# Issue order of the value products and state products in the mLSTM heads of an encoder layer

## The chip, the core and the metric

The kernel runs on one core of a Trainium2 chip. TensorE (PE) does matrix products out of SBUF into PSUM, VectorE (DVE) and ScalarE (ACT) do elementwise work, GpSimd (POOL) does masks and powers, and SyncE (SP) issues the transfers from HBM. The metric is the time of one execution on the device in microseconds.

## The reference

One encoder layer on 512 tokens of width 1024: a gated feed-forward block, a mixer, a second feed-forward block, each between RMS norms. Half of the mixer is a short convolution; the other half is four mLSTM heads, run forward and backward, in chunks of 128 tokens (q and k of width 64, v of width 128). Cut to what matters here, for one head and one direction:

```python
D = jnp.where(causal, b[..., :, None] - b[..., None, :] + li[..., None, :], NEG_INF)
...
P = jnp.exp(D - m_t[..., None]) * jnp.einsum('bhctk,bhcsk->bhcts', q, k)
inter = jnp.exp(m_inter - m_t)
numer = inter[..., None] * jnp.einsum('bhctk,bhckv->bhctv', q, C_prev) \
    + jnp.einsum('bhcts,bhcsv->bhctv', P, v)
denom = inter * jnp.einsum('bhctk,bhck->bhct', q, n_prev) + jnp.sum(P, axis=-1)
h = numer / jnp.maximum(jnp.abs(denom), jnp.exp(-m_t))[..., None]
```

For each chunk the numerator is a sum of two products: scores `P` (128x128) with values, and queries (128x64) with the state `C_prev` that the chunks before it left. The first chunk of a direction has no state. The denominator rides along as a 129th column: `v` has a column of ones, and the state its `n`.

## The kernel before, in words

Products whose operands are weights are split into a high and a low part and run in a rounded float32 type (`float32r`); the products inside the heads are plain float32, and each of them stands in the trace as two weight loads and two matmuls, so that 32 products of a line give 64 records.

The kernel is one straight program under a scheduler that keeps each engine's instructions close to the order in which they are written; which instruction waits for which follows from the tiles that they share. PSUM is a pool of eight tiles (`ps`), each one bank of 128 x 512 float32.

The mixer runs, after its projections, in this order: `head_a(0)`, `states()`, two convolution pieces, and then for each head `h` of four: `head_a(h + 1)`, `head_b(h)`, `head_c(h - 1)`, two convolution pieces. After the last of them comes the output projection (L907), then the second feed-forward block.

- `head_a(h)`: four products of keys with queries (L801, 64 rows of the PE array deep) into one PSUM tile; two products that spread gate values over rows (L806); DVE and ACT make `E`, the weighted scores of both directions (L808, L812, L814, L818).
- `states()`: the chunk states `Cs`, from weighted keys and values (L784), once for all heads.
- `head_b(h)`: for each direction `d`, into two PSUM tiles `po_` of two chunks each: the product of `E` with values (L832, 128 rows deep) for each of the four chunks, and for three of them the product of weighted queries with the state (L834, 64 rows deep: rows 0 to 63 for even heads, 64 to 127 for odd ones), accumulated onto it. DVE then forms the denominators (L841 to L844), divides (L846, L852), ACT sums squares (L857), and the head is normalized (L859).
- `head_c(h)`: four transposes (L865), the output gate (L867) and a split into high and low part.
- a convolution piece `conv(n)`: 24 products of 128 x 128 with 512 columns (L338) with a pair of weight tiles, which ACT (L220, "cast") and DVE (L221) split out of a tile `raw` that a transfer filled. The last three of the eight pieces of `w_mix_out` are loaded at L891 and split into tiles `big`.

The lines that the change touches, in short: the loop over the four chunks `c` issued for each chunk

```python
nc.tensor.matmul(o, E[...], vv[:, c, h, :], start=True, stop=i < 0)
if i >= 0:
    nc.tensor.matmul(o, qt_pair[pr][...], Cs[es, 2 * d + pr, i, :], start=False, stop=True)
```

Of the kernel before, what the change touches and what calls it, by code (L numbers as in the profile page):

```python
# [16 lines left out]
P = 128  # L17
D = 1024
S = 512
NT = S // P  # L20
# [16 lines left out]
def encoder_kernel(ctx: ExitStack, tc: tile.TileContext, a: dict, out: bass.AP):  # L37
    nc = tc.nc
# [14 lines left out]
    def nm(s):  # L53
        uid[0] += 1
        return f"{s}_{uid[0]}"
# [4 lines left out]
    def ps():  # L60
        return psum.tile([P, 512], F32, tag="ps", name=nm("ps"))

    def t2(dt=F32):
        return t2p.tile([P, 512], dt, tag="t2", name=nm("t2"))
# [4 lines left out]
    def sm(shape, dt=F32, tag="sm"):  # L69
        return small.tile(shape, dt, tag=tag, name=nm(tag))  # L70
# [4 lines left out]
    def blk(i, n=P):  # L75
        return slice(i * n, (i + 1) * n)

    def ch(v):
        return v.rearrange("p (c t) -> p c t", t=P)
# [143 lines left out]
    def rstd(parts, n, mul, tag="rs"):  # L223
        w = parts[0].shape[1]
        acc = None
        for p_ in parts:
            t = sm([P, 4], tag=tag)
            if acc is None:
                nc.vector.tensor_scalar(out=t[:, 0:w], in0=p_, scalar1=mul / n, scalar2=mul * EPS, op0=ALU.mult, op1=ALU.add)
            else:  # L230
                nc.vector.scalar_tensor_tensor(out=t[:, 0:w], in0=p_, scalar=mul / n, in1=acc, op0=ALU.mult, op1=ALU.add)  # L231
            acc = t[:, 0:w]
        r = sm([P, 4], tag=tag)
        nc.gpsimd.tensor_tensor(out=r[:, 0:w], in0=acc, in1=nhalf[:, 0:w], op=ALU.pow)  # L234
        return r[:, 0:w]
# [335 lines left out]
    vv = vaug.rearrange("p c (h e) -> p c h e", e=DV + 1)  # L571
# [138 lines left out]
    for c in range(NT):  # L710
# [3 lines left out]
        start=True, stop=True,  # L714
# [3 lines left out]
    Cs = Cf[:, 0:12 * 129].rearrange("p (q i e) -> p q i e", q=4, i=3)  # L718
# [24 lines left out]
    qt_pair = {}  # L743
# [77 lines left out]
    def head_b(h):  # L821
        pr, e = h // 2, h % 2
        es = slice(e * DK, (e + 1) * DK)
        E = hs[h]
        hsum = t2()
        for d in range(2):
            row = 32 * d + h
            po_ = [ps(), ps()]
            for c in range(NT):
                i = c - 1 if d == 0 else 2 - c  # L830
                o = po_[c // 2][:, (c % 2) * 256:(c % 2) * 256 + 129]
                nc.tensor.matmul(o, E[:, d * 512 + c * P:d * 512 + (c + 1) * P], vv[:, c, h, :], start=True, stop=i < 0)  # L832
                if i >= 0:
                    nc.tensor.matmul(  # L834
                        o, qt_pair[pr][es, d * 512 + c * P:d * 512 + (c + 1) * P], Cs[es, 2 * d + pr, i, :],
                        start=False, stop=True,
                    )
            for g in range(2):
                pov = po_[g].rearrange("p (c e) -> p c e", e=256)
                den = sm([P, 2], tag="den")  # L840
                nc.vector.scalar_tensor_tensor(  # L841
                    out=den, in0=pov[:, :, DV], scalar=-1.0, in1=nat1[:, 2 * g:2 * g + 2, 64 + row], op0=ALU.mult, op1=ALU.max)
                nc.vector.tensor_tensor(out=den, in0=pov[:, :, DV], in1=den, op=ALU.max)
                nc.vector.reciprocal(out=den, in_=den)  # L844
                if d == 0:
                    nc.vector.tensor_tensor(  # L846
                        out=ch(hsum[:, blk(g, 256)]), in0=pov[:, :, 0:DV], in1=den.broadcast_to([P, 2, DV]), op=ALU.mult,
                    )
                else:
                    for c in range(2):  # L850
                        hc = hsum[:, blk(2 * g + c)]
                        nc.vector.scalar_tensor_tensor(  # L852
                            out=hc, in0=pov[:, c, 0:DV], scalar=den[:, c:c + 1], in1=hc, op0=ALU.mult, op1=ALU.add,
                        )
        ssq = sm([P, 4], tag="ssq")
        for c in range(NT):
            nc.scalar.activation(junk[:, 0:P], hsum[:, blk(c)], AF.Square, accum_out=ssq[:, c:c + 1])  # L857
        r = rstd([ssq], DV, 1.0, tag="den4")
        nc.vector.tensor_tensor(out=ch(hsum), in0=ch(hsum), in1=r.broadcast_to([P, NT, DV]), op=ALU.mult)  # L859
        hs[h] = hsum  # L860
# [13 lines left out]
    for h in range(NH):  # L874
        if h + 1 < NH:
            head_a(h + 1)
        head_b(h)
        if h:
            head_c(h - 1)
        conv(2 * h + 3)  # L880
        conv(2 * h + 4)
# [17 lines left out]
    for tb in range(NT):  # L899
        acc = [ps(), ps()]  # L900
        for half in range(2):
            for n, k in enumerate(MIXK):
# [3 lines left out]
                for yi, wi in ((0, 0), (0, 1), (1, 0)):  # L906
                    nc.tensor.matmul(  # L907
                        acc[half], yy[yi][:, k % 4, blk(tb)], wmo[k][wi][:, blk(half, 512)],
                        start=(n == 0 and yi == 0 and wi == 0), stop=(n == 7 and yi == 1),
# [40 lines left out]
```

## Time and profile before

| | |
|---|---|
| median of 3 timed runs | 939.66 us (939.37 to 940.58) |
| profiled execution, its own time | 939.74 us |
| span of its instructions in the trace | 938.0 us |
| TensorE busy | 926.2 us of the span, 99% |
| VectorE, ScalarE, GpSimd busy | 633.5, 417.5, 39.2 us |
| granted TensorE clock, mean | 0.996 of full speed |
| the four `head_b` stretches on TensorE | 463.2 to 468.7, 481.5 to 487.0, 500.3 to 505.8, 517.3 to 522.8 us |

The span runs from the first to the last instruction in the trace; 1.7 us of the execution's own time lie outside it. Matmuls overlap, and their ends in the trace are modelled: how fast they follow each other is read from their starts, or from the chain of work that ended last, whose pieces lie end to end.

### The profile page before, as it was taken

What the parts mean: (1) busy time and instruction counts of PE and PEld (TensorE: products, weight loads), DVE (VectorE), ACT (ScalarE), POOL (GpSimd) and SP (SyncE); (2) the same over time, 40 slices, a digit from 0 to 9 for tenths busy, and PEclk for the clock granted to TensorE, in tenths of its full rate; (3) what the DMA queues carried; (4) which work ended last, traced back from release to release, by engine and by line L of the source; (5) the groups of instructions that cost most, each with busy time, mean ns of one, the idle gap of its engine ahead of it and who ended that gap; (6) DMA issues with size and microseconds to landing.
All of it is one profiled execution on the core that took longest, in us unless ns stands there. A gap on an engine that the chain in (4) does not pass through costs nothing.

```text
span 938.0 us, 14876 instructions
## 1 busy us (share of the span) xinstructions
PE 926.2 (99%) x6075; PEld 837.8 (89%) x6075; DVE 633.5 (68%) x1028; ACT 417.5 (45%) x685; POOL 39.2 (4%) x64
## 2 busy tenths in 40 slices
PE   7999999999999999999999999999999999999997
PEld 7999999999888889987777788999999999988885
DVE  5979988888822247596767636898888887942223
ACT  6655555546611234552323425554545545731111
POOL 3000000000200002000111000000000000000000
PEclk9999999999999999999999999999999999999999
DMA  8434343434332313321422500324343343443202
GB/s 257 128 91 130 100 132 91 116 110 136 118 126 94 90 46 112 91 68 51 130 68 58 167 24 9 105 73 129 92 119 106 91 135 91 157 135 89 68 6 84
DMA packets 125100, 94.35 MB, mean 101 GB/s; under 512 B 4052, under 2 KB 114664, under 8 KB 125032
## 3 DMA queue, kind: packets, MB, share of 16 engines
q1 hardware_dynamic: 125032, 93.41, 33.4%
q8 instruction: 47, 0.77, 0.3%
q14 instruction: 21, 0.17, 0.1%
HBM read 91.30 MB, written 2.10 MB: 100 GB/s over the span
## 4 chain that ended last, share of the span: by engine, by line
PE 97%; ACT 1%; issue 1%; DVE 1%; DMA 0%; POOL 0%; SPq 0%; DVEq 0%; POOLq 0%; ACTq 0%
PE ps L347 42%; PE ps L427 26%; PE ps L338 13%; PE ps L907 5%; PE ps L368 4%; PE ps L765 2%; PE ps L832 1%; PE ps L834 1%; PE ps L265 1%; DMA x<-in_x_dram 0%; PE ps L801 0%; PE ps L307 0%; ACT junk L241 0%; PE ps L784 0%; PE ps L806 0%
## 5 line engine op out<-in xcount | busy, mean ns | idle before, releaser
L221 DVE TENSOR_TENSOR wlo<-raw,whi 128x1024 fp32r<-128x1024 f32 x199 | 241.4, 1220 | 144.9 <-ACT whi L220 139.3
L220 ACT CAST whi<-raw 128x1024 fp32r<-128x1024 f32 x201 | 206.3, 1050 | 225.4 <-PE ps L427 124.2
L347 PE MATMUL ps<-big,whi 128*128 128x256 f32 x1920 | 264.5, 281 | 0.0
L347 PEld LDWEIGHTS ps<-big,whi 128*128 128x128 f32 x1920 | 243.2, 188 | 0.4
L427 PE MATMUL ps<-whi,big 128*128 128x512 f32 x704 | 221.7, 395 | 0.0
L427 PEld LDWEIGHTS ps<-whi,big 128*128 128x128 f32 x704 | 132.4, 188 | 30.9
L347 PE MATMUL ps<-big,wlo 128*128 128x256 f32 x960 | 151.0, 280 | 0.0
L427 PE MATMUL ps<-wlo,big 128*128 128x512 f32 x352 | 139.1, 395 | 0.0
L347 PEld LDWEIGHTS ps<-big,wlo 128*128 128x128 f32 x960 | 129.2, 188 | 0.0
L427 PEld LDWEIGHTS ps<-wlo,big 128*128 128x128 f32 x352 | 66.2, 188 | 15.2
L338 PE MATMUL ps<-big,whi 128*128 128x512 f32 (+1 forms) x384 | 79.7, 358 | 0.0
L338 PEld LDWEIGHTS ps<-big,whi 128*128 128x128 f32 x384 | 63.5, 188 | 10.8 <-issue 0.2
L347 PE MATMUL ps<-big,ws 128*128 128x256 f32 x480 | 65.2, 281 | 0.0
L347 PEld LDWEIGHTS ps<-big,ws 128*128 128x128 f32 x480 | 60.3, 189 | 0.0
L409 ACT COPY t<-ps 128x256 f32<-128x256 f32 x40 | 14.9, 372 | 73.4 <-PE ps L347 73.4
L338 PE MATMUL ps<-big,wlo 128*128 128x512 f32 (+1 forms) x192 | 41.2, 357 | 0.0
L241 ACT ACTIVATE junk<-ps 128x512 bf16<-128x512 f32 x24 | 14.4, 598 | 56.8 <-PE ps L427 26.8
L338 PEld LDWEIGHTS ps<-big,wlo 128*128 128x128 f32 x192 | 32.2, 188 | 5.3
L234 POOL TENSOR_TENSOR rs<-rs,nhalf 128x1 f32<-128x1 f32 x24 | 13.6, 565 | 528.2 <-DVE rs L231 528.2
L368 PE MATMUL ps<-big,whi 128*128 128x256 f32 x256 | 33.3, 282 | 0.4 <-ACT big L220 0.4
L221 DVE TENSOR_TENSOR big<-big,big 128x512 fp32r<-128x512 f32 (+1 forms) x48 | 33.0, 733 | 0.7 <-ACT big L220 0.7
L368 PEld LDWEIGHTS ps<-big,whi 128*128 128x128 f32 x256 | 31.4, 189 | 0.7 <-ACT big L220 0.6
(183 smaller groups left out, 950.7 us busy)
## 6 DMA issues: line engine op xcount, KB each, us to landing
raw<-in_w_ffn_in_dram SPq DMA_DIRECT2D x88, 512.0 KB, 4.6
raw<-in_w_ffn_out_dram SPq DMA_DIRECT2D x44, 512.0 KB, 3.5
raw<-in_w_mix_in_dram SPq DMA_DIRECT2D x24, 512.0 KB, 3.7
raw<-in_w_mix_out_dram SPq DMA_DIRECT2D x8, 512.0 KB, 3.5
out_dram<-x SPq DMA_DIRECT2D x8, 256.0 KB, 2.0
x<-in_x_dram SPq DMA_DIRECT2D x4, 256.0 KB, 4.7
x<-in_x_dram SPq DMA_DIRECT2D x2, 512.0 KB
gb<-in_norm_ffn_post_dram SPq DMA_DIRECT2D x2, 512.0 KB, 3.8
```

The source lines that it names most:

```text
L220: nc.scalar.copy(out=hi, in_=src)
L221: eng.tensor_tensor(out=lo, in0=src, in1=f32(hi), op=ALU.subtract)
L234: nc.gpsimd.tensor_tensor(out=r[:, 0:w], in0=acc, in1=nhalf[:, 0:w], op=ALU.pow)
L241: nc.scalar.activation(junk[:, 0:src.shape[1]], src, AF.Square, accum_out=s)
L265: nc.tensor.transpose(out=pt[:, blk(k)], in_=xs[:, blk(4 * b + k)], identity=ident)
L338: nc.tensor.matmul(o, ww[:, k, :], xk(xT, xx, k, sl), start=n == 0, stop=n == 3 * KD - 1)
L347: nc.tensor.matmul(o, ww[:, k, :], x[xx][:, k, :], start=first and n == 0, stop=n == 11, skip_group_check=True)
L368: nc.tensor.matmul(o, ww[:, k, :], xq_hl(xq, (k // 4, th))[xx][:, k % 4, :], start=n == 0, stop=n == 3 * KD - 1)
L409: nc.scalar.copy(a_[:, h1], x[:, h0])
L427: nc.tensor.matmul(acc[tb][half], hT[hh][:, blk(tb)], w[ww][:, blk(half, 512)], start=(k == 0 and hh == 0 and ww == 0), stop=(k == NF - 1 ...
L765: nc.tensor.matmul(pv_, xk(xT, xx, k, blk(tb)), ww[:, k % 2, :], start=n == 0, stop=n == 3 * KD - 1)
L907: nc.tensor.matmul(acc[half], yy[yi][:, k % 4, blk(tb)], wmo[k][wi][:, blk(half, 512)], start=(n == 0 and yi == 0 and wi == 0), stop=(n == ...
```

## The change

Inside `head_b`, for each direction, the loop over chunks is split into two: first the four products of scores with values, then the three products with states. Two chunks share a PSUM tile, so the accumulation flag `start` is now set on the first of the two alone; it was set for each chunk. The products, their operands and their number are the same. All lines behind L837 of the changed kernel stand four numbers higher: L834 becomes L838, L841 becomes L845, L857 becomes L861, L865 becomes L869, L891 becomes L895.

```diff
             po_ = [ps(), ps()]
+            dest = [po_[c // 2][:, (c % 2) * 256:(c % 2) * 256 + 129] for c in range(NT)]
+            before = [c - 1 if d == 0 else 2 - c for c in range(NT)]
             for c in range(NT):
-                i = c - 1 if d == 0 else 2 - c
-                o = po_[c // 2][:, (c % 2) * 256:(c % 2) * 256 + 129]
-                nc.tensor.matmul(o, E[:, d * 512 + c * P:d * 512 + (c + 1) * P], vv[:, c, h, :], start=True, stop=i < 0)
-                if i >= 0:
+                nc.tensor.matmul(
+                    dest[c], E[:, d * 512 + c * P:d * 512 + (c + 1) * P], vv[:, c, h, :],
+                    start=c % 2 == 0, stop=before[c] < 0, skip_group_check=True,
+                )
+            for c in range(NT):
+                if before[c] >= 0:
                     nc.tensor.matmul(
-                        o, qt_pair[pr][es, d * 512 + c * P:d * 512 + (c + 1) * P], Cs[es, 2 * d + pr, i, :],
-                        start=False, stop=True,
+                        dest[c], qt_pair[pr][es, d * 512 + c * P:d * 512 + (c + 1) * P], Cs[es, 2 * d + pr, before[c], :],
+                        start=False, stop=True, skip_group_check=True,
                     )
```

What this does to the order on TensorE is seen in `head_b(0)`. The rows are the built program's, one per product (x2: two alike in a row); `ps_4768` and `ps_4769` are the two PSUM tiles of the forward direction, `ps_4787` and `ps_4788` those of the backward one. Before (one more L832 row into `ps_4788` follows):

```order
L832 MATMUL ps_4768<-big_4190,t_626_4602 128x129 x2
L834 MATMUL ps_4768<-big_4445,qt_4501 128x129
L832 MATMUL ps_4769<-big_4190,t_626_4602 128x129
L834 MATMUL ps_4769<-big_4445,qt_4501 128x129
L832 MATMUL ps_4769<-big_4190,t_626_4602 128x129
L834 MATMUL ps_4769<-big_4445,qt_4501 128x129
L832 MATMUL ps_4787<-big_4190,t_626_4602 128x129
L834 MATMUL ps_4787<-big_4445,qt_4501 128x129
L832 MATMUL ps_4787<-big_4190,t_626_4602 128x129
L834 MATMUL ps_4787<-big_4445,qt_4501 128x129
L832 MATMUL ps_4788<-big_4190,t_626_4602 128x129
L834 MATMUL ps_4788<-big_4445,qt_4501 128x129
```

After:

```order
L832 MATMUL ps_4768<-big_4190,t_626_4602 128x129 x2
L832 MATMUL ps_4769<-big_4190,t_626_4602 128x129 x2
L838 MATMUL ps_4768<-big_4445,qt_4501 128x129
L838 MATMUL ps_4769<-big_4445,qt_4501 128x129 x2
L832 MATMUL ps_4787<-big_4190,t_626_4602 128x129 x2
L832 MATMUL ps_4788<-big_4190,t_626_4602 128x129 x2
L838 MATMUL ps_4787<-big_4445,qt_4501 128x129 x2
L838 MATMUL ps_4788<-big_4445,qt_4501 128x129
```

The 14 products of a head went from 13 runs of one line to 4 (of 4, 3, 4 and 3 products), and the last of them is now a state product. The other three heads read alike.

On ScalarE the scheduler moved one instruction behind the last head. Here `ssq_5233` are the sums of squares of `head_b(3)`, and `big_5394` is the high part of the last piece of `w_mix_out`:

```order
 L220 CAST big_4593<-t_741_5248 128x512
-L857 ACTIVATE junk,ssq_5233<-t_728_5192 128x128 x2
+L220 CAST big_5394<-raw_5392 128x1024
+L861 ACTIVATE junk,ssq_5233<-t_728_5192 128x128
 L220 CAST whi_5372<-raw_5370 128x1024
-L220 CAST big_5394<-raw_5392 128x1024
-L857 ACTIVATE junk,ssq_5233<-t_728_5192 128x128
+L861 ACTIVATE junk,ssq_5233<-t_728_5192 128x128 x2
 L685 COPY t_746_5283<-ps_5252 128x512
-L857 ACTIVATE junk,ssq_5233<-t_728_5192 128x128
+L861 ACTIVATE junk,ssq_5233<-t_728_5192 128x128
```

The cast of `raw_5392` now stands ahead of the first sum of squares, and so in front of the chain that ends in the normalized head. SP issues that load one place earlier too, ahead of the gains `gb_5399` instead of behind them.

On TensorE the transposes of that head (`ps_5336`) stand one product earlier inside the last convolution piece (`ps_5321`):

```order
-L338 MATMUL ps_5321<-big_3641,whi_5255 128x512 x3
-L865 MATMUL ps_5336<-ident,t_728_5192 128x128 x4
-L338 MATMUL ps_5321<-big_3641,whi_5255 128x512
+L338 MATMUL ps_5321<-big_3641,whi_5255 128x512 x2
+L869 MATMUL ps_5336<-ident,t_728_5192 128x128 x4
+L338 MATMUL ps_5321<-big_3641,whi_5255 128x512 x2
```

From there on TensorE's order is the one of before.

## Rows read from the trace of the kernel before

**Rows 1.** The page: span, TensorE busy, its granted clock, and the chain's engines.

```profile
span 938.0 us, 14876 instructions
...
PE 926.2 (99%) x6075; PEld 837.8 (89%) x6075; DVE 633.5 (68%) x1028; ACT 417.5 (45%) x685; POOL 39.2 (4%) x64
...
PEclk9999999999999999999999999999999999999999
...
PE 97%; ACT 1%; issue 1%; DVE 1%; DMA 0%; POOL 0%; SPq 0%; DVEq 0%; POOLq 0%; ACTq 0%
```

**Rows 2.** The chain in order of time, 445 to 488 us: start us, us, what.

```profile
447.38 2.79 PE ps L784 x48
450.18 11.30 PE ps L338 x48
461.48 1.09 PE ps L801 x8
462.57 0.67 PE ps L806 x2
463.23 0.45 PE ps L832 x4
463.68 0.42 PE ps L834 x2
464.09 0.42 PE ps L832 x2
...
468.27 0.42 PE ps L832 x2
468.69 11.10 PE ps L338 x48
479.79 1.08 PE ps L801 x8
...
487.00 0.44 PE ps L865 x4
```

**Rows 3.** The records of lines 832 and 834 over the whole span.

```profile
L832 PEld LDWEIGHTS ps<-big,t x64: 185/189/193, 462.8 to 522.4; 128*128 128x128 f32 x64
L832 PE MATMUL ps<-big,t x64: 272/276/379, 463.1 to 522.5; 128*128 128x129 f32 x64
...
L834 PE MATMUL ps<-big,qt x48: 272/324/375, 463.6 to 522.1; 64*128 64x129 f32 x48
```

**Rows 4.** The timeline behind the second head: start us, us, engine, line.

```profile
482.09 2.16 DVE L808 TENSOR_SCALAR t<-ps,big 128x128 f32<-128x128 f32 x8
...
487.19 3.05 PE L338 MATMUL ps<-big,whi 128*128 128x512 f32 x12
```

**Rows 5.** The timeline behind the last head, 522 to 540 us.

```profile
522.71 1.05 ACT L220 CAST big<-raw 128x1024 fp32r<-128x1024 f32 x1 [3.95 <-DMA raw<-in_w_mix_out_dram]
522.80 0.38 SPq L891 DMA_DIRECT2D raw<-in_w_mix_out_dram  x1
522.81 0.16 DVE L841 SCALAR_TENSOR_TENSOR den<-ps,big 128x2 f32<-128x2 f32 x1 [1.09 <-PE ps L832]
...
529.17 0.56 ACT L685 COPY t<-ps 128x512 f32<-128x512 f32 x1
...
529.85 0.19 ACT L857 ACTIVATION_READ_ACCUMULATOR junk<-t 128x1 f32 x1
...
532.50 0.69 DVE L859 TENSOR_TENSOR t<-t,den 128x512 f32<-128x512 f32 x1 [1.18 <-POOL den L234]
...
537.65 0.60 PE L865 MATMUL ps<-ident,t 128*128 128x128 f32 x4
```

**Rows 6.** The page's issues of transfers: the loads of the output projection.

```profile
raw<-in_w_mix_out_dram SPq DMA_DIRECT2D x8, 512.0 KB, 3.5
```

**Rows 7.** Busy time of the engines in two stretches: us, then PE, PEld, DVE, ACT, POOL.

```profile
463.00:469.00 6.00, 6.00 (x32) 4.42 (x32) 4.18 (x18) 1.26 (x2) 1.51 (x2) 1.00 0.28 87
...
523.00:538.00 15.00, 15.00 (x69) 12.19 (x68) 11.21 (x26) 6.31 (x14) 1.01 (x1) 1.00 0.63 184
```

## The prediction

> **What bounds the kernel.** I read the page first: TensorE is busy for 926.2 of 938.0 us, its granted clock reads 9 tenths or more in every slice, and the chain of work that ended last runs 97% on TensorE [rows 1]. So a microsecond saved or added on TensorE anywhere between the start and the tail is a microsecond of the whole, unless it then has to wait for somebody. Next the stretches by engine around the heads: in the first head TensorE is busy 6.00 of 6.00 us, behind the last one 15.00 of 15.00, while DVE is busy 4.18 and 11.21 [rows 7]. Nobody makes TensorE wait there. What is left is the question how long its own records take, and the chain in order of time answers it, since its pieces lie end to end [rows 2].
>
> In that chain the reader is to see two speeds for products of the same size. Four L832 records in a row (two products) take 0.45 us, 0.113 each; four transposes 0.44, 0.11 each. As soon as L832 (128 rows deep) and L834 (64 rows deep) alternate, each piece of two records takes 0.42, 0.21 per record. The column count is the same 129 [rows 3]. What differs is that the depth of the product changes between one piece and the next.
>
> **The change, part by part.**
>
> *Price of one switch.* At 0.111 a record, two records are 0.222; a piece that follows a product of the other depth takes 0.42, so a switch costs 0.42 - 0.222 = 0.198 us. A second, independent row: L801 is 64 deep, eight records in a row, with one switch into it from L338, and takes 1.08 to 1.09 [rows 2]. 1.085 - 8 x 0.111 = 0.197. If I take the L832 speed of 0.1125 instead, the two rows give 0.195 and 0.185. I use 0.195. The L801 row matters twice: it shows that products 64 deep also run at 0.111 when they follow each other, which no L834 row of before does, and that a longer run does not raise the price.
>
> *Switches per head before.* The order of `head_b(0)` has 13 runs, the first entered from L806, which is 128 deep like L832 and is no switch; the last run is L832, and what follows (L338, or the transposes L865) is 128 deep again. So 12 switches. Check: 28 records x 0.111 + 12 x 0.195 = 3.11 + 2.34 = 5.45 us; the chain runs from 463.23 to 468.69, 5.46 [rows 2].
>
> *Switches per head after.* Runs of 4, 3, 4, 3 products: three switches inside, and a fourth out of the head, since its last product is now 64 deep and the next instruction 128. 3.11 + 4 x 0.195 = 3.89 us. A saving of 8 x 0.195 = 1.56 us per head.
>
> *Sum.* Four heads: 32 switches less, 32 x 0.195 = 6.24 us. With the lowest price from rows, 0.185, it is 5.9; with the highest, 0.198, 6.3. The time of the profiled execution was 939.74, so 933.5; the median of the three runs lies 0.08 lower, within their scatter of 1.2, and I leave it at that: **933.5 us**, by the bounds 933.4 to 933.8.
>
> [...]
>
> *Flags and waits.* Setting `start` on the first chunk of a bank alone adds and removes no instruction; cost nothing. The pairs of chunks are finished at other moments: in the forward direction the first PSUM tile is complete after the fifth product instead of the third, at 8 x 0.111 + 0.195 + 2 x 0.111 = 1.31 us from the head's start, against 0.45 + 0.42 = 0.87. DVE's first L841 can so start 0.44 us later, and behind it in DVE's queue stand the score work of the next head and the convolution. The last tile of a head is complete 1.5 us earlier. Neither is waited for soon: between these scores and their use stand two convolution pieces, 11.1 us [rows 2].
>
> *What the earlier TensorE runs into.* Everything that paces it is itself paced by TensorE (casts wait for weight tiles that L338 frees), so it moves along; what does not move are gaps measured from within a head. The tightest is behind the second head: the convolution's first product takes a PSUM tile that L808 has read. All eight L808 end by 482.09 + 2.16 = 484.25, and TensorE gets there at 487.19 [rows 4]: 2.9 us to spare, 1.4 after the change. The other is the last head: its normalization ends at 533.19, its transposes run at 537.65 [rows 5], 4.4 us to spare. Here the scheduler moved the cast of the last output weights ahead of the first sum of squares. Its load was issued at 522.80, behind the gains; a load of this kind lands after 3.5 us [rows 6], so even unmoved it would land at 526.3 and the cast (1.05) would end at 527.4, 2.6 us before the last square ended (530.04), and that one stands behind the copy L685, which waits for TensorE's convolution in either order [rows 5]. The transposes stand one product earlier, 0.23 us. So I cost this edit at nothing, hidden under the 4.4 us; without that cover each microsecond late is a microsecond lost.
>
> **The rivals.**
>
> *Part of it is given back to a wait.* The spare 1.4 us behind the second head or the 4.4 behind the last one prove too little, because DVE has its work in a shorter time: it was busy 70% of the first head's stretch [rows 7], and 4.18 us of work in 6.0 - 1.56 = 4.4 leaves it nearly full. Against it: what it carries over lands in the convolution after the head, 11.1 us of TensorE [rows 2], and behind the last head DVE is idle for 3.8 us of 15 [rows 7]. If DVE fell 2 us behind in two of the heads, some 1 to 2.5 us would come back: 934.5 to 936.
>
> *The switch is not what costs.* The 0.21 per record could belong to the operands: accumulating onto a tile just written, or reading queries and states. Then 28 records at 0.21 cost 5.9 against 5.46 before, and the time is 939.7 to 941.4. For it: no row of before has L834 running alone. Against it: L832 runs at both speeds with the same operands, 0.113 in the first piece and 0.21 after, and L801 has the depth of L834 and runs at 0.111.
>
> *Slower: weight loads that no longer overlap.* Each product brings its own weights, and a run of one depth might have to wait for each load where an alternation hides it. The price: one load takes 0.189 [rows 3], and the columns take 0.058 (L784, 48 records in 2.79 us [rows 2]), together 0.247 a record; 28 x 0.247 = 6.92, 1.46 more per head, and 5.8 in all: 945.6 us. It decides as soon as a record in a run costs more than (5.46 + 0.47) / 28 = 0.212. Against it: the same three rows with 0.11 in a run, in which the load (0.189) must overlap.
>
> [...]
>
> **How the numbers follow.** The forecast (all of it, 933.4 to 933.8) has 0.84; part of it given back 0.09; the switch not being the cost 0.05; slower 0.02. The range has to leave out no more than 2 in 10: the forecast, the scatter of a median (runs of before reached 0.9 above their median), and the half of the second case gives 932.6 to 935.2. What this kernel can tell from no change is about 0.2%, 1.9 us: faster than 937.8 are the first two cases, 0.93; within 0.2% the third, 0.05; slower the last, 0.02.
>
> **What would show it.** In the chain after, each head is to read L832 x8 about 0.89, L838 x6 about 0.86, L832 x8 about 1.08, L838 x6 about 0.86, and the piece behind it 0.2 longer than before; from head start to the following L338 or transposes 3.7 us in place of 5.46. No wait of TensorE is to appear between 440 and 620 us, and the transposes of the last head are to start without one. I am wrong if a run shows 0.21 per record, if TensorE's stretches of the heads show gaps, or if the saving of 6.2 us at the heads' end has shrunk by the output projection.

## The result and the profile after

The changed kernel takes 933.61 us (median of 4 runs, 933.34 to 934.29), against 940.12 for the kernel before in its 4 runs; the ratio is 0.9932 with a 95% interval of 0.9915 to 0.9949, so it is faster. The profiled execution took 933.59 us with a span of 931.9, 6.1 us less than the span of before [rows 1]. The forecast was 933.5, in a range of 932.6 to 935.2.

The page of the kernel after: span, busy times, and the granted clock, which is the one of before.

```profile
span 931.9 us, 14877 instructions
...
PE 920.1 (99%) x6075; PEld 834.9 (90%) x6075; DVE 633.5 (68%) x1028; ACT 417.7 (45%) x685; POOL 39.2 (4%) x64
...
PEclk9999999999999999999999999999999999999999
```

All of the difference lies on TensorE, which is busy 6.1 us less. The other engines are busy as long as before, to 0.2 us. The chain in order of time (start us, us, what) of the kernel after, from the first head on:

```profile
462.74 0.67 PE ps L806 x2
463.40 0.89 PE ps L832 x8
464.29 0.86 PE ps L838 x6
465.16 1.09 PE ps L832 x8
466.25 0.86 PE ps L838 x6
467.11 11.32 PE ps L338 x48
...
483.89 0.59 PE ps L869 x4
...
534.20 21.11 PE ps L911 x91
```

This is to be read against [rows 2]. The 13 pieces of a head became four. The first L832 piece follows a product of its own depth and takes 8 x 0.111 = 0.89; the second follows a product 64 deep and takes 1.09, 0.20 more for the same eight records. A head is done in 3.71 us (463.40 to 467.11) instead of 5.46. Part of that goes to the piece behind it, which now follows a product of the other depth: L338 has 11.32 where it had 11.10, and the transposes 0.59 where they had 0.44. The output projection shows what is left. In the chain of before it began here:

```profile
540.35 21.12 PE ps L907 x91
```

From the first value product to the output projection the kernel before took 540.35 - 463.23 = 77.12 us, the one after 534.20 - 463.40 = 70.80: 6.32 us less. The spans differ by 6.1 only, since the first value product started 0.17 us later after (463.40 against 463.23), ahead of anything that the change touches. From the output projection to the end both took 397.7 us, so nothing of the saving is lost behind it.

### The profile page after: what moved, and what is told of

Same layout as the page of the kernel before. It is cut to its first block, busy times and chain, and to the rows that moved or that the text cites. A ratio compares the mean times of both kernels' runs of the same rounds, so it can differ in the third digit from the quotient of the medians.

```text
span 931.9 us, 14877 instructions
## 1 busy us (share of the span) xinstructions
PE 920.1 (99%) x6075; PEld 834.9 (90%) x6075; DVE 633.5 (68%) x1028; ACT 417.7 (45%) x685; POOL 39.2 (4%) x64
## 4 chain that ended last, share of the span: by engine, by line
PE 97%; issue 1%; DMA 1%; DVE 1%; ACT 0%; SPq 0%; DVEq 0%; POOLq 0%; POOL 0%; ACTq 0%
PE ps L347 42%; PE ps L427 26%; PE ps L338 13%; PE ps L911 5%; PE ps L368 4%; PE ps L765 2%; PE ps L265 1%; PE ps L832 1%; PE ps L838 1%; DMA gb<-in_norm_ffn_pre_dram 1%; PE ps L801 0%; PE ps L307 0%; PE ps L784 0%; PE ps L806 0%; PE ps L869 0%
## 5 line engine op out<-in xcount | busy, mean ns | idle before, releaser
L338 PE MATMUL ps<-big,whi 128*128 128x512 f32 (+1 forms) x384 | 79.8, 358 | 0.0
L338 PEld LDWEIGHTS ps<-big,whi 128*128 128x128 f32 x384 | 63.4, 188 | 11.0 <-issue 0.2
L338 PE MATMUL ps<-big,wlo 128*128 128x512 f32 (+1 forms) x192 | 41.2, 356 | 0.0
L338 PEld LDWEIGHTS ps<-big,wlo 128*128 128x128 f32 x192 | 32.2, 188 | 5.4
(183 smaller groups left out, 937.0 us busy)
```

The source lines that it names most:

```text
L338: nc.tensor.matmul(o, ww[:, k, :], xk(xT, xx, k, sl), start=n == 0, stop=n == 3 * KD - 1)
```

## Experiments

Each kernel was timed beside the kernel before, whose median was 940.05 us beside two of them (the new order at full depth, and scores and states in turn) and 940.1 beside the other four. In the diffs below `value(c, first)` and `state(c, first)` stand for the two products of chunk `c`, with their flag `start`; the other flag, `stop`, is off in both, where the change sets it on the last product of a chunk. The diffs are cut to the lines that matter. The first, the second and the fourth are against the change, the third against the second; the fifth is against the kernel before, the sixth against the fifth. The second shows the operands alone; its loop is seen in the third.

**Two changes of depth per head.** In the backward direction the states come first.

```diff
-            for c in range(NT):
-                value(c, c % 2 == 0)
-            for c in range(NT):
-                if before[c] >= 0:
-                    state(c, False)
+            if d == 0:
+                for c in range(NT):
+                    value(c, c % 2 == 0)
+                for c in (1, 2, 3):
+                    state(c, False)
+            else:
+                for c in (0, 1, 2):
+                    state(c, c % 2 == 0)
+                for c in range(NT):
+                    value(c, False)
```

> The changed kernel with one more turn: in the backward direction the three state products are issued ahead of the four value products, so that a head reads four values, six states, four values: two changes of depth per head in place of the change's four and the old twelve. Output unchanged. Theory (each change of depth costs 0.195 us, nothing else matters): 40 fewer than before, 40 x 0.195 = 7.8 us, so about 932.3 beside 940.1; the head stretch on TensorE about 3.5 us. Rival (accumulating onto a tile just written costs, depth does not): the states ahead of the values do not follow a product into their own tile, values behind them do; no gain over the change beyond 0.5 us, about 933.6.

Measured: 932.03 us (931.95 to 932.82), ratio 0.9918 (0.9904 to 0.9931): 8.1 us less than before, where the theory said 7.8, and 1.6 below the change. The chain of this kernel, first head:

```profile
463.93 0.89 PE ps L833 x8
464.83 1.53 PE ps L839 x12
466.36 1.09 PE ps L833 x8
```

The twelve state records, six of each direction, take 12 x 0.111 + 0.20 = 1.53 in one piece. That sum leaves nothing over for the two state products that open a tile: they cost as much as those that accumulate onto one.

**The old order at full depth.** The order of before, value and state in turn in one loop, but the state products over all 128 rows.

```diff
-    qt_pair[pr][es, d * 512 + c * P:d * 512 + (c + 1) * P], Cs[es, 2 * d + pr, before[c], :],
+    qt_pair[pr][:, d * 512 + c * P:d * 512 + (c + 1) * P], Cs[:, 2 * d + pr, before[c], :],
```

> The order of the kernel before, value and state in turn for each chunk, but the state products take all 128 rows of queries and states instead of the 64 of their head, so that every product of a head is 128 deep. This adds the neighbour head's state term to the output; number, columns and tiles of the products are the same. Theory (the change of depth is the cost): the alternation is free, 48 changes fewer than before, 48 x 0.195 = 9.4 us, about 930.8, with 0.111 per record in the chain. Rival (alternating operands or accumulating onto the tile just written is the cost): as before, 940.1, 0.21 per record. Rival (weight loads of one row group do not overlap): slower, above 941.

Measured: 930.79 us (930.23 to 931.15), ratio 0.9902 (0.9889 to 0.9916), 9.3 us less than before. The chain, first head and output projection:

```profile
463.80 0.45 PE ps L833 x4
464.25 0.22 PE ps L839 x2
464.47 0.22 PE ps L833 x2
464.69 0.22 PE ps L839 x2
...
531.62 21.12 PE ps L917 x91
```

Values and states alternate as they did before, state onto the tile that the value product has just written, and each piece of two records takes 0.22 where it took 0.42 [rows 2]. So neither the alternation, nor the operands, nor the accumulation costs anything. One more thing differs from the kernel before: `start` is set as in the change, on the first chunk of a tile alone. That this flag is not the cost is shown by the run grouped by tile below, which sets it in the same way and still pays at each change of depth. What costs is that the depth changes.

**The new order at full depth**, as a control: four values, three states, all 128 deep.

```diff
             for c in range(NT):
                 value(c, c % 2 == 0)
-                if before[c] >= 0:
+            for c in range(NT):
+                if before[c] >= 0:
                     state(c, False)
```

> The changed kernel's order, four values, then three states, with the state products over all 128 rows as in the run with the old order (the neighbour head's state term is added to the output). Theory: without a change of depth the order is worth nothing; the same as the old order at full depth, 930.8, within 0.5, and 9.4 us less than before. Rival (the order has a worth of its own, through the flag start, the tile just written, or DVE's earlier or later start): a difference of 1 us or more between the two orders.

Measured: 931.25 us (930.79 to 931.64), ratio 0.991 (0.9894 to 0.9927). Against the old order at full depth that is 0.46 us more, with runs that overlap, and the spans are 929.1 here and 929.3 there. The chain, first head and output projection:

```profile
463.56 0.89 PE ps L833 x8
464.45 0.67 PE ps L839 x6
...
531.39 21.11 PE ps L918 x91
```

From the first value product to the output projection that is 67.83 us, and 67.82 in the old order (463.80 to 531.62). The order has no worth of its own that these runs can tell.

**Grouped by PSUM tile only.** Eight changes of depth per head, between the change's four and the old twelve.

```diff
-            for c in range(NT):
-                value(c, c % 2 == 0)
-            for c in range(NT):
-                if before[c] >= 0:
-                    state(c, False)
+            for g in range(2):
+                for c in (2 * g, 2 * g + 1):
+                    value(c, c % 2 == 0)
+                for c in (2 * g, 2 * g + 1):
+                    if before[c] >= 0:
+                        state(c, False)
```

> Values and states grouped by PSUM tile only: two values, their states, two values, their states, in each direction. Eight changes of depth per head, four fewer than before and four more than in the change. Output unchanged. Theory: 16 fewer in all, 3.1 us, about 937.0 beside 940.1; head stretch 4.7 us. Rival (what counts is that a value run is broken at all, or the flag start on every chunk): near 940 or near 933.6, not half way.

Measured: 937.0 us (936.06 to 937.15), ratio 0.9967 (0.9955 to 0.998), as the theory gave it. In its chain a piece of four records takes 0.64, which is 4 x 0.111 + 0.195:

```profile
463.93 0.42 PE ps L839 x2
464.35 0.64 PE ps L833 x4
464.99 0.64 PE ps L839 x4
```

With these runs the price stands on a line. The third and fourth column go by the medians; the last one goes by the chain from the first value product to the output projection, 77.12 us before, and leaves out what varies outside that stretch:

| order | changes per head | us less than before | per change | by the chain |
|---|---|---|---|---|
| grouped by tile | 8 | 3.1 | 3.1 / 16 = 0.194 | 3.15 / 16 = 0.197 |
| the change | 4 | 6.5 | 6.5 / 32 = 0.203 | 6.32 / 32 = 0.198 |
| states first in the backward direction | 2 | 8.1 | 8.1 / 40 = 0.202 | 7.65 / 40 = 0.191 |
| old order, all 128 deep | 0 | 9.3 | 9.3 / 48 = 0.194 | 9.30 / 48 = 0.194 |
| new order, all 128 deep | 0 | 8.8 | 8.8 / 48 = 0.183 | 9.29 / 48 = 0.194 |

**Everything that is 64 deep put together.** The next head's gate products, then its scores, this head's six states, its eight values. `state_products` issues the six states of a head and opens their PSUM tiles; the values then accumulate onto them (not shown).

```diff
-        pS = ps()
+        pEs = [ps(), ps()]
+        for d in range(2):
+            nc.tensor.matmul(pEs[d], sel[:, 4 * d + h, :], UHL, start=True, stop=True)
+        pS = ps()
         for c in range(NT):
             nc.tensor.matmul(pS[:, blk(c)], qk[es, 2 + pr, blk(c)], qk[es, pr, blk(c)], start=True, stop=True)
+        if h:
+            state_products(h - 1)
```

> All products 64 rows deep put together: the gate products (128 deep) of the next head first, then its four score products, directly followed by the six state products of this head, then the eight value products. Output unchanged. Two changes of depth per head block, those of the scores counted: 8 in all in place of 54 before and 22 in the change. Scores and states lie in different halves of the rows, since the heads alternate. Theory with a free change of row position: 46 x 0.195 = 9.0 us less than before, about 931.1. Theory with a change of row position that costs like one of depth: 3 more, 931.7. Rival (the shorter head makes TensorE wait for DVE, since PSUM tiles are held longer): gaps on TensorE between 460 and 525 us and 932 or more.

Measured: 930.26 us (929.97 to 930.63), ratio 0.9897 (0.9882 to 0.9912): 9.8 us less than before, 0.8 more than the count of changes gave. TensorE waits for nobody between 430 and 620 us, so the rival is out. Both variants of the theory were too high, though, since they priced a change of row position at nothing or above. The timeline of TensorE shows where the rest is (L818 the scores of head 1 in rows 64 to 127, L804 the states of head 0 in rows 0 to 63):

```profile
462.56 0.82 PE L818 MATMUL ps<-big 64*128 64x128 f32 x5
463.11 0.37 PE L804 MATMUL ps<-big,qt 64*128 64x129 f32 x1
463.21 0.27 PE L818 MATMUL ps<-big 64*128 64x128 f32 x1
463.32 0.27 PE L804 MATMUL ps<-big,qt 64*128 64x129 f32 x1
463.33 0.27 PE L818 MATMUL ps<-big 64*128 64x128 f32 x1
463.44 0.27 PE L804 MATMUL ps<-big,qt 64*128 64x129 f32 x1
463.44 0.27 PE L818 MATMUL ps<-big 64*128 64x128 f32 x1
463.55 1.16 PE L804 MATMUL ps<-big,qt 64*128 64x129 f32 x9
```

From 463.11 on, state records start among the last score records, such as 463.32 beside 463.33: the two halves of the rows work at the same time. Three state records stand beside scores in this way; three of 0.111 in three heads are 1.0 us, which covers the 0.8.

**Scores and states in turn.** The same kernel, with the first four states issued between the four scores; `state_products` here returns the six products, to be issued one by one.

```diff
+        todo = state_products(h - 1) if h else []
         for c in range(NT):
             nc.tensor.matmul(pS[:, blk(c)], qk[es, 2 + pr, blk(c)], qk[es, pr, blk(c)], start=True, stop=True)
-        if h:
-            state_products(h - 1)
+            if todo:
+                todo.pop(0)()
+        for one in todo:
+            one()
```

> The run that puts states behind the scores, with the first four state products issued in turn with the four score products (they lie in different halves of the rows and write different PSUM tiles). Output unchanged. Theory (products in different halves of the rows run at the same time, which the junction of scores and states in that run showed for its last three score records): the eight score records hide wholly behind state records, some five records of 0.111 more than there in three heads, 1.3 to 1.7 us less than 930.3, about 928.8. Rival (the overlap comes once per change of half, from a load issued early, and turns cost otherwise): no gain, 930.3, or slower by 0.195 per turn, up to 7 more per head, 934.4.

Measured: 928.47 us (927.21 to 928.66), ratio 0.9876 (0.9862 to 0.9891): 1.8 less than without turns and 11.6 less than before, where the change gave 6.5. The rival, 930.3 or more, is out. The timeline, scores L821 and states L804:

```profile
462.37 0.27 PE L821 MATMUL ps<-big 64*128 64x128 f32 x1
462.38 0.27 PE L804 MATMUL ps<-big,qt 64*128 64x129 f32 x1
462.48 0.27 PE L821 MATMUL ps<-big 64*128 64x128 f32 x1
462.49 0.27 PE L804 MATMUL ps<-big,qt 64*128 64x129 f32 x1
```

Score and state start 0.01 apart, and a pair of them takes the 0.11 that one of them takes alone (462.37 to 462.48). Here a turn between the halves is not only free; it hides the scores. Five more records hidden in each of three heads are 15 x 0.111 = 1.7 us, beside 1.8 measured.

## Why the prediction was right

*What bounds.* TensorE bound the kernel and still does: it is busy 99% of the span after, and no wait of TensorE appears between 430 and 620 us. What was taken off it in the heads came out at the end.

*Price and count of the changes of depth.* The forecast was 0.195 each, 32 fewer, 6.24 us; the trace gives 6.32 between the first head and the output projection, the medians 6.5. That the time itself came within 0.1 us of the forecast is partly luck: the median of before in the result is 940.12, 0.4 above the 939.74 from which the forecast subtracted, and the medians differ by 0.3 more than the 6.24. The pieces that it named, 0.89, 0.86, 1.08 and 0.86, stand in the chain as 0.89, 0.86, 1.09 and 0.86, and the 0.2 on the piece behind the head as 11.32 against 11.10 (0.15 where the transposes follow).

*That states in a run go at 0.11 too* was read from L801, a row of another line. The chain confirms it: six records in 0.86, of which 0.195 is the change.

*Flags and waits at nothing.* Right, and the spare behind the second head came out as worked out. The timeline of the kernel after:

```profile
480.74 2.15 DVE L808 TENSOR_SCALAR t<-ps,big 128x128 f32<-128x128 f32 x8
...
484.23 2.12 PE L338 MATMUL ps<-big,whi 128*128 128x512 f32 x8
```

L808 ends at 482.89, the convolution starts at 484.23: 1.34 us to spare, where 1.4 was expected and 2.9 was there before [rows 4]. One figure of this part was off: the last tile of a head is complete 1.75 us earlier (3.71 after the head's start instead of 5.46), as the prediction's own sum has it too, and not 1.5; nothing in the forecast hung on it. Behind the last head the moved cast waited for its load, as the timeline shows:

```profile
515.78 0.33 SPq L895 DMA_DIRECT2D raw<-in_w_mix_out_dram  x1
...
520.36 1.05 ACT L220 CAST big<-raw 128x1024 fp32r<-128x1024 f32 x1 [0.53 <-DMA raw<-in_w_mix_out_dram]
...
525.55 0.69 DVE L863 TENSOR_TENSOR t<-t,den 128x512 f32<-128x512 f32 x1 [1.19 <-POOL den L234]
...
531.27 0.60 PE L869 MATMUL ps<-ident,t 128*128 128x128 f32 x4
```

From issue to cast it took 4.6 us, not the 3.5 that I had taken from [rows 6]; ScalarE stood 0.53 us for it. It did no harm, since the normalized head was ready at 526.24 and the transposes ran at 531.27, 5.0 us later; the spare before was 4.4 [rows 5].

*The rivals.* That part is given back to a wait: no wait of TensorE is there. That the change of depth is not what costs: refuted by the run of the old order at full depth, which alternates at 0.22 per product. That weight loads in a run no longer overlap: runs of up to twelve records in the same rows stand at 0.111 each, in the run with two changes per head; a load takes 0.188 (median of L838 in the kernel after), so they do overlap. The price of 0.195 us belongs to a change between 128 and 64 rows; a change between the two halves of 64 showed none in the run with scores and states in turn, where a pair of them took 0.11 us.

*What the 0.195 us looks like.* The weight loads (PEld) show where it is paid. In the kernel before, the first value products and the first state product of a head read:

```profile
463.07 0.61 PE L832 MATMUL ps<-big,t 128*128 128x129 f32 x4
463.61 0.29 PEld L834 LDWEIGHTS ps<-big,qt 64*128 64x128 f32 x2
463.61 0.49 PE L834 MATMUL ps<-big,qt 64*128 64x129 f32 x2
```

and in the same order at full depth:

```profile
463.64 0.61 PE L833 MATMUL ps<-big,t 128*128 128x129 f32 x4
463.97 0.30 PEld L839 LDWEIGHTS ps<-big,qt 128*128 128x128 f32 x2
464.08 0.39 PE L839 MATMUL ps<-big,qt 128*128 128x129 f32 x2
```

At one depth the load starts 0.33 us after the first value matmul and 0.11 ahead of its own matmul. Across a change of depth it starts 0.54 us after, 0.21 later, and no earlier than its own matmul. So the 0.11 us by which a load runs ahead of its own matmul at one depth are gone at the change of depth. Why the load starts later there stays open; the price does not grow with the length of the run before it: 0.20 us behind two state records (0.42 in the kernel before against 0.22 at full depth), 0.20 behind twelve (1.09 against 0.89 in the run with two changes).

## What to carry to other kernels

Where TensorE is the bound, look in the chain for pieces of the same size that take different times, and at the depth of the products on either side: a change between 128 and 64 rows cost about 0.195 us here (0.15 into the transposes), as much as 1.8 records of 129 columns. Group products by depth across stages and not only inside one loop, down to the fewest changes that the data allow. Then issue products that use different halves of the rows, and write different PSUM tiles, in turn: here they ran at the same time, with starts 0.01 us apart.

## What had not been expected

Products 64 deep in different halves overlapped across stages, with no effort beyond their order: four score products of one head disappeared behind the state products of another. For three heads that is 24 records of 0.111 or 2.7 us, of which the run with the states behind the scores had some 0.8 and the turns gave 1.8 more. And the shape that looks wasteful, state products over all 128 rows, half of them of no use to the head, cost less than the exact one in every order tried that leaves the scores where they stood (930.8 against 932.0 us at best); it adds the neighbour's state, so a kernel that wanted it would need zeros in that half, which was not tried.
